# First norm of a hybrid decoder step: scale and shift weights by quarters of their features, early projection blocks a quarter of k at a time

## The chip, the core and the metric

The kernel runs on one core of a Trainium2 chip. The metric is device time in microseconds (us), from one execution; lower is better. Five engines work side by side, each through its own list of instructions in order: TensorE (PE, with its weight loads shown apart as PEld), VectorE (DVE), ScalarE (ACT), GpSimd (POOL) and SyncE (SP), which here only issues transfers (DMA) from HBM. They wait for one another by semaphores.

## The reference, cut to what matters

One step of a decoder trunk for 256 prompt tokens and 8 sequences of 4 sample tokens, 288 columns in all, with D = 2048 features. Only the beginning concerns this change:

```python
mod = jax.nn.silu(c) @ P['w_ada'] + P['b_ada']           # 9 conditioning vectors, 6 x 2048 outputs
sh1, sc1, gt1, sh2, sc2, gt2 = split(mod, 6)
xn = rmsnorm(x, P['g_norm1']) * (1.0 + sc1) + sh1
proj = xn @ P['w_in']                                     # 2048 x 13336, in f32
...                                                       # three recurrent branches, merge, MLP
```

## The kernel before

Features lie on the 128 partitions, so x is 16 k-tiles of 128 features by 288 columns. A product with a large weight goes through `stream`: per **granule** (two k-tiles by 512 output columns, 512 KB of weight) SP issues one load into a tile `raw`, ACT rounds it to `hi`, DVE forms `lo` = raw - hi, and PE runs 24 matmuls of 288 columns (hi with xh, hi with xl, lo with xh, over four column tiles and two k-tiles). `raw`, `hi` and `lo` have three tiles each. The normalized activations are kept in the same way as `xh` and `xl`.

The conditioning product `silu(c) @ w_ada` goes through `cond_product`: per **load** of 1 MB, PE runs small matmuls in four column groups at once into one PSUM tile `pa`; when all loads of a product are through, DVE transposes `pa` and adds the bias into `mod`. Six kinds of 16 MB each are needed: SC1 and SH1 (scale and shift of the first norm), GT1, SH2, SC2, GT2. Those after the first piece are **fillers**: `run` takes one step of the generator `fill` (one load) behind each granule of the projections, as `pace` says.

The order at the start, before the change:

- ACT's queue issues the four loads of x, SP's the first half of SC1 (8 loads, features of k-tiles 0 to 7).
- `modulate` writes x * rstd * SC1 for that half into two scratch slots and splits it into xh and xl.
- Three blocks of 512 output columns (NPRE = 3, the first of `B_Q`) run over k-tiles 0 to 7, 4 granules each, kept in `qk` and `vv`; meanwhile the second half of SC1 comes in as fillers.
- The same three blocks run over k-tiles 8 to 15 and are added by `plus_slot`; meanwhile SH1 (16 loads) comes in.
- These 24 granules use x without its shift. `shift` then rebuilds x from xh + xl on POOL, adds SH1 and splits it again, for all 16 k-tiles; and `shift_product` (16 loads of 768 KB, again fillers) adds sh1 @ w_in to what the three blocks gave.
- All other blocks use the shifted x.

The tile scheduler sets each engine's order from the program's dependences and priorities; SP issues in its listed order and waits when a tile is not free.

Of the kernel before, what the change touches and what calls it, by code (L numbers as in the profile page):

```python
# [14 lines left out]
P = 128  # L15
D = 2048
# [9 lines left out]
NPRE = 3  # blocks of the projections before sh1  # L26

# name -> width of the constant (by shape only) and parameter columns
# [19 lines left out]
# blocks of 512 columns in the packed input projection  # L48
# [4 lines left out]
def trunk(ctx, tc, io):  # L53
# [35 lines left out]
    # ---- constants, parameters  # L89
# [37 lines left out]

    # ---- streamed weights
# [3 lines left out]
    def weight_tile(kind):  # L132
        """1024 columns: of the kind's ring, or what stands in for it: a slot or a tile of the states' ring"""
# [12 lines left out]
    def stream(w, blk, act, kt, evac, g0=0, width=512, ahead=True, k0=0):  # L146
        """k-tiles k0..kt-1; act: k -> (hi, lo); generator with a step per granule"""
# [30 lines left out]
    # ---- conditioning: silu(c) @ w_ada + b_ada  # L178
    ct, th9 = (t288()[:, 0:KT * 9].rearrange("p (k c) -> p k c", k=KT) for _ in range(2))
    Q.dma_start(ct, io["ct"])  # L180
    S.activation(th9, ct, AF.Tanh, scale=0.5)
    V.scalar_tensor_tensor(th9, th9, 1.0, ct, ALU.add, ALU.mult)
    silc = cp.tile([P, KT * 9 + 23], F32, tag="silc", name="silc")  # 9 columns a k-tile; read 32 at a time
# [6 lines left out]
    def by_feature(ps, h, n):  # L190
        """up to eight k-tiles' columns from the column groups: k-tile, 32 columns"""
# [13 lines left out]
    def cond_product(load, each, cols, stat, finish):  # L205
# [3 lines left out]
        for q in range(KT // each):  # L209
            raw = raw_tile()  # L210
            load(raw, q)
            for i in range(each):
                k = each * q + i
                v = raw[:, cols * i:cols * i + cols].rearrange("p (m j f) -> p j m f", j=4, f=32)
                for j in range(4):
                    T.matmul(ps[32 * j:32 * j + 32, 0:cols // 4], stat(k), v[:, j], start=k == 0, stop=k == KT - 1)  # L216
            if q < KT // each - 1:
# [6 lines left out]
    def ada_finish(kind):  # L224
        def finish(h, pv):
            o = mod[:, kind, 8 * h:8 * h + 8, :]
            V.tensor_tensor(out=o, in0=pv[:, :, 0:9], in1=bada[:, kind, 8 * h:8 * h + 8].unsqueeze(2).to_broadcast([P, 8, 9]), op=ALU.add)
            if kind in (SC1, SC2):  # g * (1 + sc)
                gg = Pm("g1" if kind == SC1 else "g2")
                V.scalar_tensor_tensor(o, o, 1.0, gg[:, 8 * h:8 * h + 8].unsqueeze(2).to_broadcast([P, 8, 9]), ALU.add, ALU.mult)  # L230
# [7 lines left out]
    def ada(kind):  # L238
        def load(raw, k):
            Q.dma_start(raw.rearrange("p (h m) -> p h m", h=2), wada[kind, :, k].rearrange("h p m -> p h m"))  # L240
# [8 lines left out]
    def shift_product(dst, nb):  # L249
        """the tiles of dst += sh1 @ w_in's nb blocks, for each token by its sequence"""  # L250
# [13 lines left out]
        return cond_product(load, 1, 512 * nb, lambda k: modf[:, (SH1 * KT + k) * 9:(SH1 * KT + k) * 9 + 32], finish)  # L264
# [49 lines left out]
    def modulate(xg, rs, k0, fk, xh, xl, xr):  # L314
        """k-tiles k0..k0+3 of x (xg) -> hi and lo of x * rstd * f"""
        V.tensor_tensor(out=xr, in0=xg, in1=rs.unsqueeze(1).to_broadcast([P, 4, N]), op=ALU.mult)
        bc = [P, 2, NB, TS]
        for j in range(0, 4, 2):
            r = slice(k0 + j, k0 + j + 2)
            for i in range(j, j + 2):  # L320
                V.tensor_scalar(xr[:, i, 0:NP], xr[:, i, 0:NP], mod[:, fk, k0 + i, 0:1], None, ALU.mult)
            xs = smp(xr[:, j:j + 2])
            G.tensor_tensor(out=xs, in0=xs, in1=mod[:, fk, r, 1:9].unsqueeze(3).to_broadcast(bc), op=ALU.mult)
# [937 lines left out]
```

## Time and profile before

| | us |
|---|---|
| median of 3 runs | 2063.42 |
| lowest to highest | 2063.12 to 2064.65 |
| profiled execution, its own time (span from first to last instruction) | 2058.2 |
| PE busy in it | 2000.3 (97%) |
| PE matmuls of the granules on the chain that ended last (three lines) | 24%, 23%, 23% |
| DVE, ACT, POOL busy | 1031.4, 802.4, 302.0 |

The profiled execution shows a span of 2058.2 us; the median of the runs is 5.2 us longer, since it also holds what lies around the first and the last instruction. A busy PE in this profile is not a PE at its peak: a matmul waiting in the array for its neighbour counts as busy. The stretch from 0 to 250 us is the one in which the first norm and its weights are worked on.

### The profile page before, as it was taken

How to read it: one execution, taken by the hardware profiler on the slowest of the kernel's cores; microseconds unless marked ns; L12 is line 12 of the kernel's file. 1: busy time of each engine (PE TensorE's matmuls, PEld its weight loads, DVE VectorE, ACT ScalarE, POOL GpSimd, SP SyncE). 2: the span in 40 equal slices, each digit the busy share in tenths (PEclk: the TensorE clock that was granted, in tenths of full speed). 3: DMA queues.
4: the chain of work that ended last, by engine and by line, in shares of the span. 5: the costliest groups of instructions: out<-in, count | busy, mean ns of one | idle time of the engine just before them, and what ended most of it. 6: DMA issues, size and time to landing. Idle time of an engine off the chain costs nothing.

```text
span 2058.2 us, 35340 instructions
## 1 busy us (share of the span) xinstructions
PE 2000.3 (97%) x14834; PEld 1824.4 (89%) x14834; DVE 1031.4 (50%) x1406; ACT 802.4 (39%) x1099; POOL 302.0 (15%) x342
## 2 busy tenths in 40 slices
PE   6999999999999999999999999999999999999997
PEld 4778778877889788889998989999999999999997
DVE  4354655354644366454444465434545444454565
ACT  3323465332435332244333344444343434343434
POOL 0120111021202223101111242101010101010102
PEclk8999999999999999999999999999999999999999
DMA  9988685377663257777778755555555555555552
GB/s 386 356 316 308 207 298 180 132 243 265 213 235 126 83 187 233 250 251 272 246 252 303 235 187 162 166 170 166 166 163 167 167 166 164 166 165 168 166 167 98
DMA packets 120959, 429.60 MB, mean 209 GB/s; under 512 B 11600, under 2 KB 13808, under 8 KB 120672
## 3 DMA queue, kind: packets, MB, share of 16 engines
q1 hardware_dynamic: 111728, 393.59, 56.4%
q0 software_dynamic: 7920, 29.04, 4.0%
q10 hardware_dynamic: 1152, 4.72, 0.6%
q8 instruction: 116, 1.90, 0.4%
q14 instruction: 43, 0.35, 0.0%
HBM read 410.49 MB, written 16.81 MB: 208 GB/s over the span
## 4 chain that ended last, share of the span: by engine, by line
PE 78%; DMA 2%; DVE 1%; issue 1%; POOL 1%; ACT 0%; DVEq 0%; SPq 0%; POOLq 0%
PE mm L161 24%; PE mm L163 23%; PE mm L162 23%; PE pa L216 3%; DMA st<-mC 1%; DMA ag<-wada 1%; DVE lo L155 0%; PE px L658 0%; PE pi L974 0%; PE px L931 0%; PE pi L535 0%; PE px L125 0%; PE px L980 0%; PE px L555 0%; DMA o_C_s<-st 0%
## 5 line engine op out<-in xcount | busy, mean ns | idle before, releaser
L155 DVE TENSOR_TENSOR lo<-raw,hi 128x1024 fp32r<-128x1024 f32 (+1 forms) x424 | 543.0, 1283 | 616.9 <-ACT hi L154 603.7
L154 ACT ACTIVATE hi<-raw 128x1024 fp32r<-128x1024 f32 (+1 forms) x424 | 442.9, 1046 | 801.5 <-PE mm L162 663.2
L161 PE MATMUL mm<-xh,hi 128*128 128x288 f32 x2168 | 645.4, 300 | 12.0 <-ACT xh L341 5.5
L162 PE MATMUL mm<-xl,hi 128*128 128x288 f32 x2168 | 641.3, 297 | 1.2 <-DVE xl L342 1.2
L163 PE MATMUL mm<-xh,lo 128*128 128x288 f32 x2168 | 630.2, 297 | 1.2 <-DVE lo L155 1.2
L161 PEld LDWEIGHTS mm<-xh,hi 128*128 128x128 f32 x2168 | 406.9, 188 | 67.5 <-issue 37.8
L163 PEld LDWEIGHTS mm<-xh,lo 128*128 128x128 f32 x2168 | 404.6, 189 | 13.4 <-issue 8.1
L162 PEld LDWEIGHTS mm<-xl,hi 128*128 128x128 f32 x2168 | 408.5, 188 | 8.8 <-issue 6.9
L162 PE MATMUL mm<-s,hi 128*128 128x288 f32 x1176 | 348.1, 296 | 0.0
L161 PE MATMUL mm<-s,hi 128*128 128x288 f32 x1176 | 347.6, 297 | 0.0
L163 PE MATMUL mm<-s,lo 128*128 128x288 f32 x1176 | 345.0, 295 | 0.0
L161 PEld LDWEIGHTS mm<-s,hi 128*128 128x128 f32 x1176 | 220.6, 188 | 13.6 <-issue 11.8
L163 PEld LDWEIGHTS mm<-s,lo 128*128 128x128 f32 x1176 | 220.9, 188 | 2.4 <-issue 2.2
L162 PEld LDWEIGHTS mm<-s,hi 128*128 128x128 f32 x1176 | 221.3, 188 | 1.2 <-issue 0.9
L1102 POOL TENSOR_TENSOR t<-t 128x288 f32<-128x288 f32 x64 | 62.6, 989 | 638.9 <-ACT t L1101 638.9
L161 PE MATMUL mm<-s,st 128*128 128x288 f32 x488 | 143.9, 296 | 0.0
L162 PE MATMUL mm<-s,st 128*128 128x288 f32 x488 | 143.3, 294 | 0.0
L154 ACT ACTIVATE st<-s 128x1024 fp32r<-128x1024 f32 x80 | 84.7, 1059 | 131.0 <-PE mm L162 86.9
L161 PE MATMUL mm<-xh,st 128*128 128x288 f32 x408 | 120.5, 297 | 0.2 <-DVE xl L1088 0.2
L162 PE MATMUL mm<-xl,st 128*128 128x288 f32 x408 | 120.1, 295 | 0.0
L161 PEld LDWEIGHTS mm<-s,st 128*128 128x128 f32 x488 | 91.7, 188 | 0.8 <-ACT t L296 0.8
L162 PEld LDWEIGHTS mm<-s,st 128*128 128x128 f32 x488 | 91.9, 188 | 0.0
(369 smaller groups left out, 2104.6 us busy)
## 6 DMA issues: line engine op xcount, KB each, us to landing
raw<-win SPq DMA_DIRECT2D x192, 512.0 KB, 4.4
raw<-wf SPq DMA_DIRECT2D x176, 512.0 KB, 3.4
ag<-wada SPq DMA_DIRECT2D x57, 1024.0 KB, 6.1
s<-wf SPq DMA_DIRECT2D x80, 512.0 KB, 3.5
s<-wada SPq DMA_DIRECT2D x39, 1024.0 KB, 8.3
raw<-wout SPq DMA_DIRECT2D x32, 512.0 KB, 4.4
s<-win SPq DMA_DIRECT2D x11, 768.0 KB, 7.2
st<-mC POOLq DMA_DIRECT2D x16, 514.0 KB, 4.6
```

The lines of the kernel that those rows point to most:

```text
L154: S.activation(hi, raw, AF.Copy)
L155: V.tensor_tensor(out=lo, in0=raw, in1=hi.bitcast(F32), op=ALU.subtract)
L161: T.matmul(pss[m][:, :N], hi[:, kk, ms], xh, start=k == k0, stop=False)
L162: T.matmul(pss[m][:, :N], hi[:, kk, ms], xl, start=False, stop=False)
L163: T.matmul(pss[m][:, :N], lo[:, kk, ms], xh, start=False, stop=k == kt - 1)
L216: T.matmul(ps[32 * j:32 * j + 32, 0:cols // 4], stat(k), v[:, j], start=k == 0, stop=k == KT - 1)
L1102: G.tensor_tensor(out=r, in0=r, in1=r, op=ALU.mult)
```

## The change

- The weights of SC1 and SH1 are stored anew (`wada1`) and multiplied by quarters of their output features: one product is 4 loads, each of four k-tiles by 512 features, 128 columns a matmul, and each partition's row of a load is 8 KB in one piece. The order is SC1 q0; SC1 q1; SC1 q2, SH1 q2; SC1 q3, SH1 q3; SH1 q0; SH1 q1.
- x is loaded on SP's queue ahead of the weights, and is multiplied by rstd in place, all four quarters at once.
- `modulate(q)` scales quarter q in place and, in quarters 2 and 3 (`LATE` = 2 and up), adds the shift in the same pass.
- The three early blocks run over k a quarter at a time: 2 granules for each block, 6 for a quarter. Quarters 1 to 3 are added by `plus_slot`.
- `shift(q)` is left for quarters 0 and 1 and works on x in place; POOL's sum of xh and xl is gone. `shift_product` runs over k-tiles 0 to 7 alone: 8 loads, not 16.
- An extra activation `warm` on ACT at the start; GT1, SH2, SC2 and GT2 get a plain layout (8 KB rows).

```diff
+    xa, xb = slot(0), slot(1)
+    xq = [(xa, xb)[q // 2][:, 4 * (q % 2):4 * (q % 2) + 4, :] for q in range(4)]
     Q.dma_start(ct, io["ct"])
+    for q in range(4):
+        Q.dma_start(xq[q], io["x"][:, 4 * q:4 * q + 4, :])
...
+    S.activation(sc([P, 1], "warm", 1), eps, AF.Sqrt)
...
-    def ada_half(kind, h):
-        """eight of the k-tiles of one kind"""
-        def load(raw, q):
-            Q.dma_start(raw.rearrange("p (k m) -> p k m", k=2), wada[kind, h, 2 * q:2 * q + 2].rearrange("k p m -> p k m"))
-        return cond_product(load, 2, 1024, silu_c, lambda _, pv: ada_finish(kind)(h, pv))
+    def ada_quarter(kind, q):
+        def load(raw, g):
+            Q.dma_start(raw, io["wada1"][kind, q, g])
+        return cond_product(load, 4, 512, silu_c, lambda _, pv: ada_finish(kind, 4)(q, pv))
...
     def fillers():
-        yield from ada_half(SC1, 1)
-        done.add("sc")
-        yield from ada(SH1)
+        for q in range(1, 4):
+            yield from ada_quarter(SC1, q)
+            if q >= LATE:
+                yield from ada_quarter(SH1, q)
+            modulate(q)
+            done.add(q)
+        for q in range(LATE):
+            yield from ada_quarter(SH1, q)
+            shift(q)
         done.add("sh")
-        yield from shift_product((qk, vv), NPRE)
+        yield from shift_product((qk, vv), NPRE, 4 * LATE)
...
-    def shift(k0, shk, xh, xl, xr):
-        h, l = xh[:, k0:k0 + 4, :], xl[:, k0:k0 + 4, :]
-        G.tensor_tensor(out=xr, in0=h.bitcast(F32), in1=l.bitcast(F32), op=ALU.add)
+    def shift(q):
+        k0, x = 4 * q, xq[q]
+        with tc.high_priority():
+            by_seq(x, SH1, k0, ALU.add)
...
-    for i in range(4):
-        t = (xa, xb)[i // 2]
-        S.dma_start(t[:, 4 * (i % 2):4 * (i % 2) + 4, :], io["x"][:, 4 * i:4 * i + 4, :])
...
-    slots["ids"] = 2, 4, 5, 6, 7, 8, 9, None
-    all_of(ada_half(SC1, 0))
-    xs3, xs4 = slot(3), slot(4)
+    slots["ids"] = 2, 3, 4, 5, 6, 7, None
...
+    all_of(ada_quarter(SC1, 0))
+    modulate(0)
...
-    for b in range(NPRE):
-        run(stream(win, B_Q + b, act1, 8, to_slot((qk, vv)[b // 2], 4 * (b % 2)), ahead=b > 0))
-    drain("sc")
-    scale1(1)
-    for b in range(NPRE):
-        run(stream(win, B_Q + b, act1, KT, plus_slot((qk, vv)[b // 2], 4 * (b % 2)), k0=8))
+    for q in range(4):
+        if q:
+            drain(q)
+        for b in range(NPRE):
+            ev = plus_slot if q else to_slot
+            run(stream(win, B_Q + b, act1, 4 * q + 4, ev((qk, vv)[b // 2], 4 * (b % 2)), ahead=q > 0, k0=4 * q))
     drain("sh")
-    for i in range(4):
-        shift(4 * i, SH1, xh, xl, (xs3, xs4)[i % 2][:, 0:4, :])
```

What this makes of the order shows at three places. The first is SP's queue at the start. The destinations are `s..` (a slot), `ag` (the ring tile) and `raw`. Before:

```order
L180 DMA t288_1_89<-ct 128x144
L246 DMA s4_24_159<-wada 128x2x1024
...
L246 DMA ag_30_219<-wada 128x2x1024
L246 DMA s2_31_229<-wada 128x2x1024
L153 DMA raw_41_275<-win 128x1024
L153 DMA raw_46_316<-win 128x1024
```

and after:

```order
L185 DMA s0_1_89<-x 128x1152 x2
L185 DMA s1_2_90<-x 128x1152 x2
L257 DMA s3_27_167<-wada1 128x2048
...
L257 DMA s6_30_221<-wada1 128x2048
L154 DMA raw_36_258<-win 128x1024
L257 DMA s7_40_289<-wada1 128x2048
L154 DMA raw_41_307<-win 128x1024
L257 DMA ag_44_341<-wada1 128x2048
L154 DMA raw_49_363<-win 128x1024
```

Four loads of weights, not eight, now stand ahead of the first granule's `raw`, and x stands ahead of all of them.

The second is PE's list where the thirteenth granule of the early blocks begins (`pa` is the conditioning product; the first `mm` rows are the granule). Before, it follows the fifth load of SH1:

```order
L163 MATMUL mm_82_615<-xh1_104,lo_98_727 128x288
L216 MATMUL pa_86_646<-s2_99_759,silc_94 32x512 x4
L216 MATMUL pa_86_646<-s5_107_821,silc_94 32x512 x4
L161 MATMUL mm_100_787<-xh1_104,hi_105_792 128x288
L162 MATMUL mm_100_787<-xl1_105,hi_105_792 128x288
```

and after:

```order
L164 MATMUL mm_100_797<-xh1_106,lo_107_848 128x288
L225 MATMUL pa_152_1278<-s7_161_1331,silc_102 32x128 x11
L225 MATMUL pa_152_1278<-ag_165_1383,silc_102 32x128 x16
...
L225 MATMUL pa_178_1497<-s5_191_1602,silc_102 32x128 x16
L225 MATMUL pa_178_1497<-s6_192_1620,silc_102 32x128 x16
L162 MATMUL mm_112_930<-xh1_106,hi_117_935 128x288
```

All 32 loads of SC1 and SH1 now stand ahead of the thirteenth granule on PE; before, 21 stood ahead of it (16 of SC1, 5 of SH1) and 11 of SH1 behind it. On SP the same place reads, after:

```order
L257 DMA s5_191_1602<-wada1 128x2048
L257 DMA s6_192_1620<-wada1 128x2048
L154 DMA raw_116_934<-win 128x1024
L154 DMA raw_120_982<-win 128x1024
```

The granule's `raw` (`raw_116`) is the 48th transfer of the list and follows the last load of SH1.

The third is POOL's list where the shift is made. Before:

```order
L329 TENSOR_TENSOR s3_33_243<-xh1_104,xl1_105 128x1152
L329 TENSOR_TENSOR s4_34_244<-xh1_104,xl1_105 128x1152
L425 DMA s5_263_2108<-lst 128x192
L333 TENSOR_TENSOR s3_33_243<-s3_33_243,mod_97 128x4x32
...
L446 DMA s3_261_2105<-lruw 128x2048
```

and after:

```order
L334 TENSOR_TENSOR s1_2_90<-s1_2_90,mod_105 128x4x32 x4
L334 TENSOR_TENSOR s0_1_89<-s0_1_89,mod_105 128x4x32
L460 DMA s3_298_2495<-lruw 128x2048
L439 DMA s5_300_2498<-lst 128x192
L334 TENSOR_TENSOR s0_1_89<-s0_1_89,mod_105 128x4x32
```

The sums of 1152 columns are gone, and the 1 MB load `lruw` now stands between the shift of quarter 0 and that of quarter 1.

## Rows read from the trace of the kernel before

**Rows 1.** The page: PE's line (busy us, share, instructions) and the granted clock in 40 slices.

```profile
PE 2000.3 (97%) x14834; PEld 1824.4 (89%) x14834; DVE 1031.4 (50%) x1406; ACT 802.4 (39%) x1099; POOL 302.0 (15%) x342
...
PEclk8999999999999999999999999999999999999999
```

**Rows 2.** Stretches: us, busy (instructions) of PE, PEld, DVE, ACT, POOL, clock, DMA, GB/s.

```profile
10.00:20.00 10.00, 8.47 (x69) 4.96 (x69) 3.06 (x19) 5.16 (x11) 0.00 (x0) 1.00 1.02 411
20.00:30.00 10.00, 5.53 (x66) 2.57 (x68) 4.58 (x3) 0.50 (x1) 0.00 (x0) 0.91 1.02 408
30.00:40.00 10.00, 3.87 (x32) 1.60 (x24) 6.44 (x15) 5.50 (x7) 2.90 (x6) 0.50 1.02 408
40.00:50.00 10.00, 8.85 (x62) 7.96 (x60) 5.28 (x7) 0.07 (x1) 0.00 (x0) 0.74 1.02 409
...
46.00:97.00 51.00, 51.00 (x433) 39.59 (x431) 18.03 (x26) 18.44 (x28) 8.93 (x6) 1.00 0.96 358
```

**Rows 3.** Instructions in order of time: start, us, engine, line, what, [idle before <-releaser].

```profile
32.79 1.06 ACT L154 ACTIVATE hi<-raw 128x1024 fp32r<-128x1024 f32 x1 [10.89 <-DMA raw<-win]
...
38.98 1.33 PE L161 MATMUL mm<-xh,hi 128*128 128x288 f32 x4 [5.51 <-ACT xh L341]
...
50.56 1.06 ACT L154 ACTIVATE hi<-raw 128x1024 fp32r<-128x1024 f32 x1 [10.49 <-DMA raw<-win]
```

**Rows 4.** Stretches from granule to granule, all instructions, columns as in rows 2.

```profile
38.97:97.18 58.21, 57.05 (x456) 45.12 (x456) 24.52 (x33) 19.71 (x30) 8.93 (x6) 0.95 0.96 363
97.19:137.96 40.77, 40.77 (x308) 30.95 (x305) 15.45 (x24) 7.97 (x8) 2.52 (x4) 1.00 0.97 368
137.97:245.86 107.89, 105.40 (x794) 93.22 (x793) 60.04 (x75) 42.04 (x55) 14.01 (x15) 1.00 0.72 238
198.81:208.40 9.59, 9.59 (x74) 9.59 (x73) 3.68 (x3) 3.19 (x3) 0.00 (x0) 1.00 0.53 165
```

**Rows 5.** The first three of them for line L216 alone: PE, PEld, clock, DMA, GB/s.

```profile
38.97:97.18 58.21, 14.64 (x168) 4.36 (x168) 0.95 0.96 363
97.19:137.96 40.77, 11.17 (x92) 2.04 (x88) 1.00 0.97 368
137.97:245.86 107.89, 13.81 (x120) 3.41 (x120) 1.00 0.72 238
```

**Rows 6.** PE's waits between 138 and 170 us, columns as in rows 3.

```profile
147.36 0.40 PE L163 MATMUL mm<-xh,lo 128*128 128x288 f32 x1 [0.82 <-DVE lo L155]
...
153.00 0.37 PE L161 MATMUL mm<-xh,hi 128*128 128x288 f32 x1 [1.18 <-DVE s L380]
...
168.82 0.40 PE L161 MATMUL mm<-xh,hi 128*128 128x288 f32 x1 [0.46 <-ACT hi L154]
```

**Rows 7.** The shift on POOL and DVE, columns as in rows 3.

```profile
141.37 3.58 POOL L329 TENSOR_TENSOR s<-xh,xl 128x1152 f32<-128x1152 f32 x1 [3.13 <-DVE xl L342]
...
142.34 3.83 DVE L342 TENSOR_TENSOR xl<-s,xh 128x1152 fp32r<-128x1152 f32 x1
```

**Rows 8.** Transfers issued from 0 to 160 us: count, KB each, median us to landing.

```profile
s<-wada SPq DMA_DIRECT2D x26, 1024.0 KB, 8.9
raw<-win SPq DMA_DIRECT2D x30, 512.0 KB, 7.7
...
s<-x ACTq DMA_DIRECT2D x4, 576.0 KB, 7.4
...
con<-con POOLq DMA_DIRECT2D x1, 422.0 KB, 6.8
par<-par POOLq DMA_DIRECT2D x1, 213.0 KB, 6.7
```

**Rows 9.** Queues from 20 to 28 us, then 160 to 170: packets, MB, engines' share.

```profile
q1 hardware_dynamic: 837, 3.24, 101.3%
...
q0 software_dynamic: 144, 1.05, 25.0%
```

**Rows 10.** Groups by line, 96 to 160 us: count | busy us, mean ns | idle before.

```profile
L380 DVE TENSOR_TENSOR s<-s,mm 128x288 f32<-128x288 f32 x12 | 5.2, 450 | 13.2 <-PE mm L163 12.9
```

More of the change, by code (lines that the diff above doesn't have):

```diff
@@ L26 @@
 NPRE = 3
+LATE = 2
 CONSTS = [("ident", 128), ("eye", 32), ("bcol", 8), ("smask", 32), ("slo", 32), ("shi", 32),
@@ L176, in run @@
                 next(fill, None)
-    ct, th9 = (t288()[:, 0:KT * 9].rearrange("p (k c) -> p k c", k=KT) for _ in range(2))
+    xa, xb = slot(0), slot(1)
+    xq = [(xa, xb)[q // 2][:, 4 * (q % 2):4 * (q % 2) + 4, :] for q in range(4)]
+    ct = t288()[:, 0:KT * 9].rearrange("p (k c) -> p k c", k=KT)
     Q.dma_start(ct, io["ct"])
+    for q in range(4):
+        Q.dma_start(xq[q], io["x"][:, 4 * q:4 * q + 4, :])
+    th9 = t288()[:, 0:KT * 9].rearrange("p (k c) -> p k c", k=KT)
     S.activation(th9, ct, AF.Tanh, scale=0.5)
+    S.activation(sc([P, 1], "warm", 1), eps, AF.Sqrt)
     V.scalar_tensor_tensor(th9, th9, 1.0, ct, ALU.add, ALU.mult)
@@ L203, in raw_tile, with cond_product @@
         return flat(slot(i))[:, 0:2048]
-    def cond_product(load, each, cols, stat, finish):
+    def cond_product(load, each, cols, stat, finish, kt=KT):
         ps = pa.tile([P, 512], F32, tag="pa", name=nm("pa"))
-        for q in range(KT // each):
+        for q in range(kt // each):
             raw = raw_tile()
@@ L215, in cond_product @@
                 for j in range(4):
-                    T.matmul(ps[32 * j:32 * j + 32, 0:cols // 4], stat(k), v[:, j], start=k == 0, stop=k == KT - 1)
-            if q < KT // each - 1:
+                    T.matmul(ps[32 * j:32 * j + 32, 0:cols // 4], stat(k), v[:, j], start=k == 0, stop=k == kt - 1)
+            if q < kt // each - 1:
                 yield
@@ L263, in finish @@
             G.tensor_tensor(out=d, in0=d, in1=o[:, :, 1:9].unsqueeze(3).to_broadcast([P, n, NB, TS]), op=ALU.add)
-        return cond_product(load, 1, 512 * nb, lambda k: modf[:, (SH1 * KT + k) * 9:(SH1 * KT + k) * 9 + 32], finish)
+        return cond_product(load, 1, 512 * nb, lambda k: modf[:, (SH1 * KT + k) * 9:(SH1 * KT + k) * 9 + 32], finish, kt)
     def all_of(g):
@@ L312, in smp @@
         return a[..., NP:N].rearrange("p k (b t) -> p k b t", b=NB)
[L314 to L323, printed above, removed]
-            split(xh[:, r, :], xl[:, r, :], xr[:, j:j + 2])
@@ new lines, in modulate @@
+    def modulate(q):
+        k0, x = 4 * q, xq[q]
+        with tc.high_priority():
+            by_seq(x, SC1, k0, ALU.mult)
+            if q >= LATE:
+                by_seq(x, SH1, k0, ALU.add)
+            for j in range(0, 4, 2):
+                for i in range(j, j + 2):
+                    f, sh = (mod[:, kind, k0 + i, 0:1] for kind in (SC1, SH1))
+                    if q >= LATE:
+                        V.tensor_scalar(x[:, i, 0:NP], x[:, i, 0:NP], f, sh, ALU.mult, ALU.add)
+                    else:
+                        V.tensor_scalar(x[:, i, 0:NP], x[:, i, 0:NP], f, None, ALU.mult)
+                r = slice(k0 + j, k0 + j + 2)
+                split(xh[:, r, :], xl[:, r, :], x[:, j:j + 2])
@@ L336, in split @@
+    def shift(q):
+        k0, x = 4 * q, xq[q]
+        with tc.high_priority():
+            by_seq(x, SH1, k0, ALU.add)
+            for i in range(4):
+                V.tensor_scalar(x[:, i, 0:NP], x[:, i, 0:NP], mod[:, SH1, k0 + i, 0:1], None, ALU.add)
+            split(xh[:, k0:k0 + 4, :], xl[:, k0:k0 + 4, :], x)
     def split(dst_h, dst_l, src):
@@ L360, in trunk @@
     rs = rstd_of(ps)
+    for q in range(4):
+        V.tensor_tensor(out=xq[q], in0=xq[q], in1=rs.unsqueeze(1).to_broadcast([P, 4, N]), op=ALU.mult)
     def act1(k):
@@ L381, in plus_slot @@
         return f
-    def scale1(h):
-        t = (xa, xb)[h]
-        for i in range(2):
-            with tc.high_priority():
-                modulate(t[:, 4 * i:4 * i + 4, :], rs, 8 * h + 4 * i, SC1, xh, xl, (xs3, xs4)[i % 2][:, 0:4, :])
-    slots["ids"] = 2, 5, 6, 7, None
-    scale1(0)
+    all_of(ada_quarter(SC1, 0))
+    modulate(0)
     G.tensor_copy(con[:, 0:1], mod[:, SC1, 0, 0:1])
@@ L394, in trunk @@
     pace["every"] = (1,)
[L395 to L400 removed]
+    for q in range(4):
+        if q:
[3 more added lines that the diff above has]
+            run(stream(win, B_Q + b, act1, 4 * q + 4, ev((qk, vv)[b // 2], 4 * (b % 2)), ahead=q > 0, k0=4 * q))
     drain("sh")
[L402 to L403 removed]
     pace["every"] = (1, 0)
```

25 lines of the change are left out of this document (12 added, 13 removed).

## The prediction

> **What bounds the kernel now.** I read the page first: PE is busy 97% of the span and the granted clock stands below 9 only in the first of the 40 slices [rows 1]. So nothing can come back except idle PE time, slow-clock time, or PE work that is left out. Next the stretches [rows 2]. From 10 to 50 us the DMA column stands at 1.02 and 408 to 411 GB/s while PE is half idle at 20 to 40 and the clock goes down from 0.91 to 0.50: the start waits for transfers. From 46 to 97 us PE is busy in all 51.00 us and DMA runs at 358 GB/s, below what it has just shown: now PE is the bound. The first granule begins at 38.98, after 5.51 us of idleness [rows 3]. From there to 97.18 the weight loads number 456, of which 168 are the conditioning product's [rows 4, 5]; 288 are left, twelve granules of 24. So the thirteenth granule begins at 97.19, and I use it as the milepost: what comes after it is nearly the same in both kernels, and what PE still owes there can be counted.
>
> **What one piece costs.** Three granules without fillers take 9.59 us, 3.20 each [rows 4]. From 97.19 to 137.96 there are nine granules (28.8 us) and 88 weight loads of the product, 8 for a load of SH1, so 11 loads [rows 4, 5]: (40.77 - 28.8) / 11 = 1.09 us of PE each. From 137.97 to 245.86 there are 28 granules (89.5 us), 15 loads of the shift product, and the three waits of 0.82, 1.18 and 0.46 us [rows 4 to 6]: (107.89 - 89.5 - 2.5) / 15 = 1.06 us each.
>
> **Transfers.** The landing of a transfer in a saturated queue can be counted by bytes. Before, the first `raw` has behind it x and c (2.43 MB), the parameters (0.22), eight loads of 1.05 and its own 0.52 [rows 8], 11.56 MB; at 0.409 MB/us that is 28.3 us, and ACT takes it up at 32.79 [rows 3]: 4.5 us on top. The `raw` of 50.56 [rows 3] has 18.81 MB: 46.0 + 4.5 = 50.5. So landing = 4.5 + MB / 0.409, as long as SP never lets the queue run dry.
>
> **The change, part by part.**
>
> *A smaller first piece.* Four loads instead of eight ahead of the first granule. The fifth load (first of SC1 q1) stands ahead of it on PE, 8.4 MB, lands at 25; with its 1.09 us and the scaling, the first granule begins at about 27, 12 us earlier. This is no gain yet.
>
> *The milepost moves to the transfers.* Ahead of the thirteenth granule PE now owes twelve granules and 27 loads after the first granule's start: 38.4 + 29.4 = 68 us, so PE could be there at 95. But the granule's `raw` is the 48th transfer, behind all 32 loads: 2.43 + 0.22 + 0.43 + 32 x 1.05 + 13 x 0.52 = 43.45 MB, 106.2 + 4.5 = 110.7, and with 1.06 us of ACT [rows 3] 111.8. The transfers are later by some 16 us, and they decide; all that the early part does on PE, DVE, ACT or POOL (extra activation, smaller transposes, seven ends of products that wait for DVE) lies in those 16 us and costs nothing unless it exceeds them.
>
> *Two corrections to 111.8.* The new loads have one row of 8 KB a partition. The only such load in the trace took 25.0% of 10 us for 1.05 MB, 2.50 us, where those of the first half of SC1 took 101.3% of 8 us for 3.24 MB, 2.62 per load [rows 9]: between 0 and 32 x 0.12 = 3.8 us earlier; I take 2, since the row is of POOL's queue. And `lruw` (1.05 MB) now goes out between the shifts of q0 and q1, when the last loads are still under way: between 0 and 2.6 us later; I take 1. So the thirteenth granule begins at 110.8 (108 to 114.5).
>
> *What PE no longer owes there.* Before, at 97.19, there were still 11 loads of SH1 (12.0 us), 16 of the shift product, of which 8 are dropped (8.5 us), and the waits of 2.5 us. The first two of these lie where DVE is held up: the xl of 1152 columns takes 3.83 us beside POOL's sum of 3.58 [rows 7]; the sums are gone, so I count all three waits as gone. The same state is reached before at 97.2 + 12.0 + 8.5 + 2.5 = 120.2.
>
> *New waits behind the milepost.* 24 more additions by `plus_slot` at 0.45 us [rows 10] are 10.8 us of DVE work, on an engine half idle, but PE's next block needs the PSUM tile that they empty. The `raw` of the sixteenth granule can be issued only when the thirteenth's `lo` is made, and lands about when PE wants it. No row shows these; the nearest are the waits of 0.46 to 1.18 us [rows 6]. Bounds 0 and 4 us; I take 2.0.
>
> *Sum.* 120.2 - 110.8 - 2.0 = 7.4 us. Everything later has the same granules and fillers and I cost it at nothing. Against the profiled execution: 2058.2 - 7.4 = 2050.8. The median of the runs is 5.2 us above that execution's span, so 2063.4 - 7.4 = **2056.0**.
>
> **The clock.** The trace shows the granted clock at 0.50 (the 1.2 GHz level) at 30 to 40 us, after PE had been busy 5.53 of 10 us, and 0.74 at 40 to 50, when the granules ran without a gap [rows 2]. Now PE waits for transfers between 27 and 111, with 68 us of work in 84. Slow work there eats the 16 us of slack first. The Trainium skill ("TensorE: Matmul & The Clock Gate", section "HAM oscillation — how this bites in real kernels") says that a kernel whose bursts of matmuls are shorter than the waits for data between them starts every burst at the low clock. By that rule the pieces of this stage would each run at half speed; the trace agrees for the one such stretch that it has, and it is the third rival.
>
> **The rivals.**
>
> 1. *The queue has holes and the gain is given back.* SP issues in order, and a load waits for its tile; with seven tiles the twenty-sixth load waits for PE to finish the nineteenth. By my count SP is some 12 us ahead there, so the queue should not run dry, but the trace before does show 358 GB/s as soon as tiles bind [rows 2]. At a mean of 390, 43.45 MB take 111.4 us, the milepost is at 117.0, the gain 1.2: 2062.
>
> 2. *Slower: the holes are as before.* If this stage gets the 358 GB/s of 46 to 97 us [rows 2], the milepost is at 121.4 + 4.5 + 1.1 = 127.0 and the kernel 8.8 us slower: 2072. It decides from 43.45 / (118.2 - 5.6), 386 GB/s, downwards. Against it: 40 us on end at 408 and more, with the same sizes. The Trainium skill ("DMA: Bandwidth & Descriptors", section "Where 436 GB/s comes from") gives about 358 GB/s as HBM's limit for one core and says that it binds transfers from HBM; by it the time would be the same 2072. The rows of 10 to 50 us exceed it, so it adds little to the chance.
>
> 3. *PE at half clock.* If the clock stays at half for more than about 16 us of PE work (at full clock) between 27 and 111, PE decides the milepost and not the transfers; and if it is down at the milepost, the granules there take 6.4 us instead of 3.2 until it is back. Slack used up and 3 us more at each end: about 2066. For it: the busy share of 20 to 30. Against: work of 68 in 84 us, and a PE that falls behind is a PE without gaps.
>
> **How the numbers follow.** Forecast 0.70 (2051 to 2060), rival 1 0.16, rival 2 0.09, rival 3 0.05. A measurement of this kernel tells some 0.2%, 4.1 us, from no change. Faster than 2059.3: nearly all of the forecast and a third of rival 1, 0.74. Within 0.2%: most of rival 1, some of the forecast and of rival 3, 0.13. Slower: rival 2 and the rest, 0.13. The range runs from all corrections in favour (milepost 108, no new waits: 12 us, 2051) to rival 1, 2050.5 to 2063.
>
> **What would show it.** Right: the first granule near 27; DMA above 400 GB/s from 10 to about 105; the thirteenth granule near 111 and its `hi` released by DMA, with PE idle or product-only in the 10 us ahead; three waits of [rows 6] gone, no sum on POOL. Wrong: GB/s below 390 in that stretch (rivals 1, 2); a clock under 0.9 from 50 to 110 (rival 3); waits of PE behind DVE of more than 4 us between 111 and 250.

## The result: slower, and the profile after

The median of 20 runs is 2070.0 us, against 2063.6 for 20 runs of the kernel before on the same chip: the ratio is 1.0033 with an interval of 1.0020 to 1.0046, about 6.8 us slower. The forecast was 2056.0, and faster. The profiled execution of after has a span of 2060.8 us and took 2062.6, so 1.8 us lie around the span, and it is one of the shortest of its set. Against the 2058.2 of before it is 2.6 us longer. Both numbers are needed below: 2.6 us between the two traces, and between the sets of runs 6.4 by the medians or 6.8 by the ratio.

The page, to be held against [rows 1]: PE's line and the granted clock.

```profile
PE 1997.6 (97%) x15410; PEld 1846.6 (90%) x15410; DVE 1034.8 (50%) x1430; ACT 804.4 (39%) x1099; POOL 286.4 (14%) x334
...
PEclk9999999999999999999999999999999999999999
```

PE is busy 2.7 us less, in a span that is longer. The start is no longer slow. Stretches with the columns of [rows 2]:

```profile
20.00:30.00 10.00, 5.33 (x73) 4.64 (x74) 9.55 (x15) 3.27 (x4) 1.29 (x3) 0.76 1.02 419
...
46.00:97.00 51.00, 42.65 (x650) 38.18 (x651) 23.15 (x41) 14.37 (x21) 1.99 (x4) 1.00 1.02 417
...
46.00:110.00 64.00, 52.42 (x884) 46.97 (x888) 27.68 (x51) 15.53 (x22) 3.65 (x7) 1.00 1.02 417
110.00:120.00 10.00, 6.83 (x51) 6.56 (x40) 5.82 (x10) 4.34 (x4) 0.74 (x2) 0.66 1.03 392
```

From 46 to 97 us, where PE had been busy all the time, it is now busy 42.65 of 51 us and the transfers run at 417 GB/s, faster than in any row of [rows 2]. At the milepost the clock is at half: 0.66 is the mean of 10 us in which it stood at 0.50 from 110.6 to 117.4. The first granule, the thirteenth, and the `hi` for which the latter waits, as in [rows 3]:

```profile
27.69 0.61 PE L162 MATMUL mm<-xh,hi 128*128 128x288 f32 x1 [0.42 <-ACT xh L367]
...
112.43 1.06 ACT L155 ACTIVATE hi<-raw 128x1024 fp32r<-128x1024 f32 x1 [6.21 <-DMA raw<-win]
...
113.54 0.61 PE L162 MATMUL mm<-xh,hi 128*128 128x288 f32 x1 [3.17 <-ACT hi L155]
```

The chain is as forecast (transfer, `hi`, granule, PE idle ahead of it), 2.7 us later. How SP issues these transfers, in order of time (start, us, operation, tile, count):

```profile
60.24 9.11 SPq L257 DMA_DIRECT2D s<-wada  x5
70.28 4.04 SPq L154 DMA_DIRECT2D raw<-win  x3
...
82.09 7.30 SPq L257 DMA_DIRECT2D s<-wada  x5
90.24 5.30 SPq L154 DMA_DIRECT2D raw<-win  x3
```

Loads and granules stand in **bursts**: five or more loads, then three granules (three `raw` tiles), then loads again. The code is written with one load between two granules; the order came out this way because the loads have seven tiles and the granules three. So all 32 loads stand ahead of the thirteenth granule, which the prediction knew and counted. What it did not weigh is what bursts do to PE: it waits for a load, then works them all off, then waits for a `raw`. Waits of PE from 46 to 120 us (who for whom, us in all, times, longest):

```profile
PE mm L162 <- ACT hi L155: 6.5, 4, 3.2
PE pa L225 <- DMA s<-wada: 5.3, 4, 1.8
PE pa L225 <- DVE s L347: 1.5, 1, 1.5
```

And granule to granule for all instructions, then for the product's line alone, as in [rows 4] and [rows 5]:

```profile
113.53:254.98 141.45, 141.44 (x1008) 124.28 (x1009) 74.09 (x110) 48.70 (x62) 8.56 (x13) 0.99 0.68 233
...
113.53:254.98 141.45, 19.46 (x120) 3.81 (x120) 0.99 0.68 233
```

From the thirteenth to the fiftieth granule (254.99; before 97.19 to 245.87) PE never waits: the waits of [rows 6] and the sum of [rows 7] are gone. But 37 granules of 3.20 are 118.4 us, and 120 weight loads of the product are 15 loads, so these took (141.45 - 118.4) / 15 = 1.54 us each, where before they took 1.07.

### The profile page after: what moved, and what is told of

Its sections match the earlier page's. It is cut to its first block, busy times and chain, and to the rows that moved or that the text cites. A ratio compares the mean times of both kernels' runs of the same rounds, so it can differ in the third digit from the quotient of the medians.

```text
span 2060.8 us, 36520 instructions
## 1 busy us (share of the span) xinstructions
PE 1997.6 (97%) x15410; PEld 1846.6 (90%) x15410; DVE 1034.8 (50%) x1430; ACT 804.4 (39%) x1099; POOL 286.4 (14%) x334
## 4 chain that ended last, share of the span: by engine, by line
PE 89%; DMA 5%; DVE 2%; issue 2%; ACT 1%; POOL 1%; DVEq 0%; SPq 0%; POOLq 0%; ACTq 0%
PE mm L162 27%; PE mm L164 26%; PE mm L163 26%; PE pa L225 4%; DMA raw<-win 3%; DMA st<-mC 1%; DVE lo L156 1%; DMA ag<-wada 1%; DMA s<-wada 1%; PE pi L381 1%; PE px L672 0%; PE px L945 0%; PE pi L549 0%; PE pi L988 0%; ACT hi L155 0%
```

## How runs are compared

Two runs of one kernel differ by 15 us and more, and each run's record holds its span and its mean granted clock. Span times clock estimates what the run would have taken at 2.4 GHz throughout; the rest of the span is put down to stretches at 1.2 GHz. That splits a mean over runs into two parts. The split is rough. Within one kernel span times clock still spreads by 2.4 us (standard deviation over all sets), where the spans spread by 3.6. And it counts half clock at which PE has nothing to do: in each profile 3.9 to 5.4 us of the loss lie in the last 8 to 11 us, behind PE's last matmul, and cost nothing. All ratios are to the kernel before on the same chip. "Steps" and "tiles" are explained with the experiments.

| kernel | ratio, interval | mean span | lost to clock | at full clock |
|---|---|---|---|---|
| before (four sets of 23 to 35) | 1 | 2059.9 to 2062.3 | 19.8 to 21.3 | 2040.1 to 2040.9 |
| before_again | 1.0005, 0.9992 to 1.0018 | 2061.0 | 20.6 | 2040.4 |
| after | 1.0033, 1.0020 to 1.0046 | 2067.8 | 24.5 | 2043.3 |
| after_again | 1.0028, 1.0016 to 1.0040 | 2066.0 | 23.4 | 2042.6 |
| late4 | 1.0036, 1.0020 to 1.0052 | 2066.4 | 20.7 | 2045.7 |
| warm1 | 1.0048, 1.0030 to 1.0065 | 2069.8 | 21.7 | 2048.1 |
| tiles3 | 1.0001, 0.9986 to 1.0015 | 2060.2 | 24.4 | 2035.8 |
| steps8 | 1.0010, 0.9997 to 1.0024 | 2061.5 | 21.3 | 2040.2 |
| tie | 1.0018, 1.0001 to 1.0035 | 2063.9 | 20.8 | 2043.1 |
| mix | 0.9983, 0.9970 to 0.9995 | 2056.1 | 23.3 | 2032.8 |
| mix_tie | 0.9974, 0.9957 to 0.9991 | 2055.6 | 19.2 | 2036.4 |
| lruw_late | 1.0012, 0.9998 to 1.0026 | 2063.1 | 23.7 | 2039.4 |
| mix_late4 | 0.9963, 0.9950 to 0.9977 | 2053.3 | 13.9 | 2039.5 |
| mix8 | 0.9933, 0.9914 to 0.9952 | 2047.5 | 20.5 | 2027.0 |
| mix8, second set | 0.9926, 0.9900 to 0.9952 | 2046.9 | 18.4 | 2028.5 |
| steps_gt2 | 1.0015, 1.0003 to 1.0028 | 2065.6 | 22.0 | 2043.5 |
| norm_warm | 1.0030, 1.0017 to 1.0043 | 2068.2 | 23.6 | 2044.6 |

A difference of 1 to 1.5 us in a part of a row is within what sets of the same kernel show (2040.1 to 2040.9 and 19.8 to 21.3 for before, 2042.6 and 2043.3, 23.4 and 24.5 for after; the two sets of six runs of mix8 differ by 2.1 in the clock). Between after and before, 1.7 to 3.2 us are work and waits and 2.1 to 4.7 are clock, as the sets are paired; after_again and the before beside it on one chip give 2.5 and 3.6.

## The experiments

### The two kernels once more

before_again and after_again have no edit.

> The kernel before, unchanged, run again for its own spread and for a second profile. Medians so far: before 2063.6 us, after 2070.0 us. Clock theory: the runs of after differ from one another by their mean granted clock (0.984 gave 2076, 0.991 gave 2061.7 to 2067.8), and the profiled run of before had 0.991; so before's runs should lie near 0.990 to 0.991 in the mean, after's near 0.988, and at equal clock the two kernels should differ by less than 2 us. Rival, later waits: the clocks are alike, and after is some 6 us longer at equal clock. Second profile: no stretch at half clock between 90 and 130 us nor between 300 and 360 us, if the ones of after belong to after.

> The kernel after, unchanged, beside the others of this call: is it as long on this chip, and does its clock loss come again? Spans of after so far: 2067.8 us in the mean at a mean granted clock of 0.9881, of before 2060.4 at 0.9904; span times (1 - clock) is what half speed costs: 24.5 us for after, 19.8 for before, so 4.7 us of the 7.4 us between them is clock and 2.8 us is work and waits. If that belongs to the kernel: 2068 to 2071.5 us, clock 0.987 to 0.989, and a wait of 4.2 us near 1223 us, with no load beside it. If it belonged to the chip and the hour: within 2 us of before.

Measured: 2063.3 us at a mean clock of 0.9900, and 2068.2 at 0.9887. The slowdown belongs to the kernel. At full clock the two are 1.7 to 3.2 us apart: the clock theory (under 2) has the larger part of the difference, but not all of it. The second profile of before has no half-clock stretch from 90 to 130 or 300 to 360 us, as expected; the second of after has them again at 111, 309 and 347 us.

### late4: the second part of the change undone

```diff
-LATE = 2
+LATE = 4
```

> The kernel after with the shift in none of the quarters: all of it goes through the product of the shift with the blocks, 16 loads of that product instead of 8. The prediction's price for the 8 loads is 8 x 1.06 = 8.5 us of TensorE; with after at 2070.0 us it gives 2076 to 2080 us, the 13th granule within 2 us of 113.5 us, since the same 32 loads stand ahead of it. Rival, the second part is hidden or is given back later in waits: 2068 to 2073 us.

Measured: 2067.4 us, ratio 1.0036, thirteenth granule at 112.74. The rival holds: eight more loads of the shift product make after no longer by anything that can be measured in the total. By the table late4 is 2.4 to 3.1 us longer at full clock and loses 2.7 to 3.8 us less to the clock. What the prediction counted as 8.5 us isn't there in this kernel's time, and the first part of the change alone is 7 us slower than before.

### tiles3 and mix: no bursts

tiles3 gives the loads three tiles instead of seven; mix gives the first four loads tiles of their own, and those behind them three.

```diff
-    slots["ids"] = 2, 3, 4, 5, 6, 7, None
+    slots["ids"] = 4, 5, 6, 7
...
     all_of(ada_quarter(SC1, 0))
+    slots["ids"] = 2, 3, None
```

> The kernel after with three tiles instead of seven for the loads of the scale, shift and shift product while the early blocks run: the program's row then has about one load between two granules, and only some 14 loads ahead of the 13th granule instead of 32. Bunching theory (loads queued in bursts of five to seven ahead of the granules' own weights make the stretch to 113 us bound by transfers): the 13th granule between 78 and 95 us, no wait for a load over 2 us between 50 and 90, and 2045 to 2058 us in all, faster than both kernels. Clock theory alone (only half-clock stretches cost): the half-clock stretch at the milepost goes, 2 to 5 us less than after, 2064 to 2068 us. Later-stage theory (the loss is behind 250 us, whatever comes ahead): 2067 to 2073 us, with the same half-clock stretches near 310 and 350 us after the shift in time.

> As tiles3, but the four loads of the first scale quarter have four tiles of their own, and the loads behind them three: tiles3's first granule started at 34.3 us instead of 27.7, since its fourth load waited for a tile. Bunching theory: first granule at 27.5 to 28.5, no burst of loads, the 13th granule at 82 to 88, and 5 to 6.5 us less than tiles3 (2062.9): 2056 to 2058.5 us. Rival (transfers bind after all once the start is earlier, 28 transfers ahead of the 13th granule at 413 GB/s would be there by 70 us): 2060 to 2063 us.

Measured: tiles3 2062.9 us, thirteenth granule at 91.20; mix 2058.0, at 86.04, first granule at 28.5. SP now issues in single file. The lines are those of mix8, below, which has mix's order here:

```profile
56.23 0.33 SPq L154 DMA_DIRECT2D raw<-win  x1
59.70 0.33 SPq L257 DMA_DIRECT2D ag<-wada  x1
60.12 0.86 SPq L154 DMA_DIRECT2D raw<-win  x2
64.87 3.92 SPq L257 DMA_DIRECT2D s<-wada  x2
```

At full clock mix stands 10 us below after, and the forecast gain of 7.4 us over before is there (2032.8 against 2040.4). And mix begins its fiftieth granule at 246.17, 8.8 us ahead of after, with the same loads left to do. So the bursts are one cause, and the larger one. The edit changes two things together, the waits between bursts and the number of loads ahead of the milepost (17 instead of 32), and no run tells these apart. tiles3's expected time was missed by 5 us, since its fourth load waits for a tile and its first granule starts at 34.34; mix mends that and gains the 5 us, as expected. But mix still loses 23.3 us to the clock, as after does: single file doesn't cure that.

### warm1: is it the clock at the milepost?

One product of 288 columns that nothing reads, behind each of the last 16 loads:

```diff
+            if warm:
+                T.matmul(misc()[:, :N], ones, raw[:, 0:N], start=True, stop=True)
```

> The kernel after with one more product of 128x128 with 288 columns, whose result nothing reads, behind each of the last 16 loads of the scale and shift (16 x about 0.5 = 8 us of TensorE, in a stretch of 46 us that holds about 36 us of work). Clock theory: no half-clock stretch at 110 to 117 us, the 13th granule within 2 us of 113.5, and 2 to 4 us less than after by 160 us; in all 2064 to 2069 us if the later stretches stay as they are. Rival, the clock there doesn't depend on how busy TensorE was, or the extra products delay the granules: half clock all the same, 2070 to 2076 us. Bunching theory: the milepost itself doesn't move, since transfers bound it.

Measured: 2072.1 us, thirteenth granule at 112.33. The half-clock stretch at the milepost is gone; another comes at 134.6, behind a new wait:

```profile
110.00:120.00 10.00, 9.38 (x101) 7.63 (x93) 7.28 (x13) 4.16 (x4) 1.46 (x3) 1.00 1.03 399
130.00:140.00 10.00, 6.78 (x32) 4.69 (x33) 2.84 (x6) 0.94 (x1) 0.00 (x0) 0.83 0.97 344
```

The loss to the clock falls by some 2 us and the time at full clock rises by 5, so the expected gain did not come; the median lies in the rival's range. The milepost itself is where the bytes put it.

### lruw_late: the bytes ahead of the milepost

A copy of one column holds the LRU's weights back:

```diff
+        G.tensor_copy(flat(wax)[:, 0:1], flat(lx)[:, 0:1])
         G.dma_start(flat(wax)[:, 0:2048], io["lruw"])
```

> The kernel after with the transfer of the LRU's weights (1.05 MB, which runs beside the loads on POOL's queue ahead of the 13th granule) held back until the LRU's projection is out, by a copy of one column. Size theory: the milepost is bound by the sum of the bytes, so the 13th granule starts 2 to 2.6 us earlier, at 110.8 to 111.5 instead of 113.5 us, and the median falls by no more than that, 2067 to 2070 us. Rival (that transfer doesn't compete): 113.5 and the time of after within 1 us.

Measured: thirteenth granule at 111.44, 2.1 us earlier than in after and 1.3 earlier than in after_again; the size theory holds there. The median is 2064.1, ratio 1.0012, some 3 to 4 us below after, more than expected. In its profile PE waits 1.35 instead of 3.17 us at the milepost and no half-clock stretch follows there. But another one stands at 64.9 to 71.7, and over its runs the loss to the clock is that of after (23.7); the table has the 3 to 4 us at full clock (2039.4). What makes up more than the 2.1 us stays open.

### steps8 and steps_gt2: where the later loads stand

The eight dropped loads leave a row that is shorter by eight: every later load (GT1, SH2, SC2, GT2) stands eight granule steps earlier than before. steps8 puts eight empty steps in their place and changes no work; steps_gt2 puts them only ahead of GT2.

```diff
         done.add("cor")
+        for _ in range(8):
+            yield
```

> The kernel after with eight empty steps in the row of fillers, behind the shift product and ahead of the loads of the later scales: the loads that follow stand at the granules at which they stood in the kernel before, which had eight loads more ahead of them. Nothing of the work changes. Later-stage theory (the dropped loads pull the later ones forward, onto the stage of the LRU, and the waits and half-clock stretches of after between 300 and 355 us come from that): the waits on DVE L533 fall from 3.33 and 3.01 us to the 2.2 and 2.5 us of before, the half-clock stretches near 308 to 319 and 350 us go, and the median is 2062 to 2066 us. Rival (the stage's waits don't depend on where the loads stand): 2068 to 2072 us.

> The kernel after with the eight empty steps of steps8 only ahead of the loads of the last scale, so that everything up to some 900 us stands as in after, and only the second norm near 1220 us has loads again beside its wait. steps8 took 5.3 to 7 us off after; this tells its two parts apart. Cover theory (the loads are missing at the second norm): the wait there falls from 4.2 us to some 2.7, with 2.8 loads beside it, 2.0 to 2.5 us at full clock and up to 3.4 us of clock: 2063 to 2066.5 us. Rival (the stage of the LRU and the GLA, 290 to 600 us, had the gain, by where the loads stand there): 2067 to 2070 us.

Measured: steps8 2062.9 us, ratio 1.0010, 4 to 5 us below after, as expected; but not where I expected it. Its waits from 285 to 360 us, in the LRU's stage, fell only from 7.4 to 6.2 us in all: PE waited 3.9 us behind DVE at 295 us, with a half-clock stretch behind it. What the traces show is the second norm. Before, PE's row there (start, us, instructions, [idle before]):

```profile
1215.34 0.63 PE L216 MATMUL pa<-s,silc 128*32 128x512 f32 x3
1215.36 0.62 PE L216 MATMUL pa<-ag,silc 128*32 128x512 f32 x1
1215.79 0.61 PE L216 MATMUL pa<-s,silc 128*32 128x512 f32 x3
1215.81 1.44 PE L216 MATMUL pa<-ag,silc 128*32 128x512 f32 x7
...
1218.26 1.62 PE L300 MATMUL pi<-t,ones 128*128 128x288 f32 x6
1222.36 1.56 PE L216 MATMUL pa<-ag,silc 128*32 128x512 f32 x8 [2.48 <-DMA ag<-wada]
1224.08 1.33 PE L161 MATMUL mm<-xh,st 128*128 128x288 f32 x4 [0.15 <-DVE xl L1088]
```

and after:

```profile
1219.17 0.75 PE L317 MATMUL pi<-t,ones 128*128 128x288 f32 x2
...
1220.64 1.24 PE L317 MATMUL pi<-t,ones 128*128 128x288 f32 x4 [0.23 <-ACT t L313]
1222.35 0.75 PE L317 MATMUL pi<-t,ones 128*128 128x288 f32 x2 [0.47 <-ACT t L313]
1227.31 1.33 PE L162 MATMUL mm<-xh,st 128*128 128x288 f32 x4 [4.21 <-ACT xh L1101]
```

Before, 22 matmuls of the product (2.75 loads) stood around the norm's chain of ACT and DVE, and PE waited 2.6 us; after, the loads had run out before it, and PE waited 4.9 us with nothing else to do. The code says so: ahead of the norm it asks for three more loads, and after the change there are none left to give. In steps8 they are back, and PE waits 2.7 us. The dropped loads had been **cover** for this wait.

steps_gt2 restores just that: the 22 matmuls are back and PE waits 2.41 us. Its median is 2068.6 us, in the rival's range (the kernel before had 2063.5 on that chip). By its ratio, 1.0015, it is some 3 us below after, the size that the cover theory gave; yet the split by clock puts none of it at full clock (2043.5), and the interval touches that of after. (The 5.3 to 7 us for steps8 in its expectation are differences of medians from different chips; by the ratios they are 4 to 5.) So the row shows 2.3 to 2.5 us at the norm; how much of it reaches the end, and what the rest of steps8 is, stays open.

### tie and mix_tie: the waits of the LRU's stage

Waits of PE from 290 to 360 us, in before and then in after:

```profile
PE mm L161 <- DVE s L519: 4.8, 2, 2.5
```

```profile
PE mm L162 <- DVE s L533: 6.3, 2, 3.3
PE px L593 <- DMA s<-wg: 1.1, 1, 1.1
```

DVE's four scans of 1.34 us stand in a row ahead of the next `lo` and of the instruction of L533 that PE waits for, in after:

```profile
302.43 5.09 DVE L513 TENSOR_TENSOR_SCAN s<-s,s 128x576 f32<-128x576 f32 x4
```

tie holds them back with copies of one column until granules of the gate are out:

```diff
+                V.tensor_copy(flat(hh)[:, 2 * h * N:2 * h * N + 1], (sm[:, 0:1], sg[:, 0, 0:1], sg[:, 4, 0:1], sg[:, 4, 0:1])[h])
                 V.tensor_tensor_scan(flat(hh)[:, r], flat(aa)[:, r], flat(thi)[:, r], 0.0, ALU.mult, ALU.add)
```

> The kernel after with the four scans of the LRU (1.34 us of DVE each, in one row ahead of the lo of the next granules) held back by copies of one column until granules of the gate have come out, so that the lo stands between them. It tests what the waits at 305 and 345 us cost, with their half-clock stretches. Clock theory (the half-clock stretches at 308 to 319 and 350 us follow from these waits): both waits under 1 us, the stretches gone, 2043.3 us at full clock fall by 4 to 6 and the loss of clock of 24.5 us by some 5: 2059 to 2063 us. Rival (half-clock stretches come elsewhere instead): the waits go alone, 2064 to 2067 us. Second rival (the scans only delay something else as much): 2068 to 2072 us.

> mix and the held-back scans of tie together. If the bursts of loads and the waits of the LRU stage are two separate causes, their gains add: mix's 5 to 6.5 us below tiles3 and some 4 to 11 us for the scans, 2046 to 2054 us, faster than both kernels. If the clock takes back what the waits gave, 2055 to 2058 us, as mix alone.

Measured: tie 2066.1 us, mix_tie 2057.9. The stretch is cured:

```profile
300.00:320.00 20.00, 20.00 (x139) 14.79 (x138) 12.68 (x23) 5.66 (x8) 1.12 (x2) 1.00 0.80 302
...
365.00:380.00 15.00, 13.10 (x91) 12.02 (x90) 9.05 (x7) 10.18 (x16) 4.23 (x3) 0.89 0.57 209
```

PE is busy 20.00 of 20 us at full clock where after had two half-clock stretches. But a new wait of 1.9 us, with a half-clock stretch, stands at 366, and the time at full clock is that of after (2043.1); only the loss to the clock is 3 us less. For mix the scans bring nothing: 4 us less clock, 4 us more work and waits. The two expectations of a full gain fell; tie came out where the first rival had it (stretches come elsewhere instead), mix_tie at mix alone.

### mix8 and mix_late4: both mended, and the price of the dropped loads

mix8 is mix with the eight empty steps, mix_late4 is mix with LATE = 4.

> mix (loads not in bursts) with the eight empty steps of steps8 (the loads of the later scales stand where before had them). mix alone: 2058.0 us, of which 2032.8 us at full clock and 23.3 us lost to the clock; it waits 4.2 us at the second norm (1217 to 1222 us) with no load left there, where before had 22 weight loads of the product in the same stretch and waited 2.5 us. Cover theory (loads that were dropped had covered waits further on): 2.3 us less wait there, and the clock loss back towards 20 us: 2051 to 2056 us, faster than all others. Rival (the two edits mend the same loss): 2057 to 2059 us.

> mix with the whole shift through the product with the blocks, 16 loads instead of 8: the price of the second part of the change where no burst and no transfer hides it. A whole load of that product takes 0.78 us of TensorE in the traces, so 8 are 6.2 us, or up to 8 us where they stand cut in pieces; less the 2.3 us that they cover at the second norm: 2061 to 2064 us at mix's clock. Rival (as with late4 against after, the loads cost nothing in the sum): 2056 to 2059 us.

> mix8 once more, word for word, for an interval of its own: its first set held only six runs. If the gains of the loads in single file and of the eight steps add, 2047 to 2051 us, some 13 us below before and 20 below after, at a clock loss near 20.5 us as in before; if the first set was a lucky one, 2052 to 2056 us.

(The last of these ran mix8 unchanged, as its text says; the label names another edit.) Measured: mix8 2048.7 and 2049.8 us, ratios 0.9933 and 0.9926: **14 us faster than before and some 20 faster than after**, the best of all. mix_late4 is 2055.8, ratio 0.9963, 5 us below what I expected, just under the rival's range. The same product, eight loads more or less, has these prices:

- later loads eight steps too early: late4 to after, 1.0036 to 1.0033 and 1.0028, and mix_late4 to mix, 0.9963 to 0.9983: from 1.6 us gained to 4 us lost;
- later loads in their place: late4 to steps8, 1.0036 to 1.0010, and mix_late4 to mix8, 0.9963 to 0.9933 and 0.9926: 5.4, 6.2 and 7.6 us gained.

So the second part of the change is worth 5 to 8 us, near its forecast, but in the total only if what follows keeps its place. Where it does not, the clock takes the gain: at full clock the pairs of the first line give 2.4, 3.1 and 6.7 us gained, those of the second 5.5, 11.0 and 12.5. And mix differs from mix_late4 in more than the place of later loads. Its profile has a wait of 3.0 us for a load at 112.7, with half clock from 115.0 to 121.8 behind it; mix_late4's is busy 68.49 of the 70 us from 60 to 130, all at full clock. PE's waits in mix8 from 50 to 130 us, to be held against after's above:

```profile
PE pa L225 <- DVE s L349: 1.5, 1, 1.5
PE pa L225 <- DVE t L202: 0.9, 1, 0.9
PE pa L225 <- DMA s<-wada: 0.8, 1, 0.8
PE mm L162 <- ACT xh L369: 0.8, 1, 0.8
```

### norm_warm: does filling a wait save clock?

Five products that nothing reads, behind the second norm's reciprocal:

```diff
+    for _ in range(5):
+        T.matmul(misc()[:, :N], ones, rs, start=True, stop=True)
```

> The kernel after with five products of 128x128 with 288 columns, whose result nothing reads, behind the second norm's reciprocal, in its wait of 4.2 us (5 x 0.62 = 3.1 us): TensorE has something to do there, but no work is saved. Clock theory (the half-clock stretch at 1227 us follows from the idle time ahead of it): no half-clock stretch between 1220 and 1235 us, 1.7 to 3.4 us less lost to the clock, 2065 to 2068 us. Rival (what the idle time does to the clock is small or the half-clock stretch comes elsewhere): 2068 to 2071 us.

Measured: 2070.4 us, ratio 1.0030, as after. PE still waits 2.58 us, for the reciprocal, and the clock is down from 1231.0 all the same:

```profile
1228.27 0.75 PE L317 MATMUL pi<-t,ones 128*128 128x288 f32 x2 [0.46 <-ACT t L313]
...
1231.61 1.81 PE L1088 MATMUL px<-row,ones 128*128 128x288 f32 x3 [2.58 <-DVE row L325]
```

The median lies in the rival's range, and the clock theory gets nothing from this run; since part of the wait stayed, it isn't refuted either.

## Why the prediction was wrong, step by step

**The first granule, the rate, the chain: right.** Near 27 was forecast, 27.69 came. The transfers were to run above 400 GB/s from 10 to 105; they ran at 413 to 422 (stretches of 10 us, and 417 from 46 to 110). At that rate a load with 8 KB rows comes to 1.05 MB / 417 GB/s = 2.51 us, as the row of POOL's queue had shown [rows 9]. Rivals 1 and 2 fell with it: the queue had no holes. The page that spoke for rival 2, the Trainium skill's "DMA: Bandwidth & Descriptors", section "Where 436 GB/s comes from", gives about 358 GB/s as the limit of HBM for one core; the trace has 417 over 51 us, and the measurement decides.

**"So the thirteenth granule begins at 110.8": 2.7 us too early.** 113.54 lies inside the bounds that stood beside it (108 to 114.5). Holding `lruw` back gave 2.1 against after and 1.3 against after_again (112.75): that transfer took half or more of the possible 2.6, where I had counted 1.

**"Slow work there eats the 16 us of slack first": right up to the milepost, then wrong.** The third rival's second half came true at the worst place: the clock was at 0.50 from 110.6 to 117.4, just when the granules began. From 113.54 on that is 3.86 us at half, 1.9 us lost. Of the page of the Trainium skill named there, "TensorE: Matmul & The Clock Gate", section "HAM oscillation — how this bites in real kernels", the trace bears out no more than this stretch: from 46 to 110 us PE was idle 11.6 of 64 us, in waits between bursts, and the clock was 1.00. That 1.00 is in part this profile's luck: late4, steps8, lruw_late, steps_gt2 and norm_warm load in the same bursts there, and each has 3.4 to 6.8 us at half clock between 65 and 73 us. The prediction named the case that came (the clock down at the milepost), but it gave both halves of the rival one price, 2066, and one chance, 0.05, and none of it stands in the sum.

**"12.0 and 8.5 us", loads at 1.07 us each whatever their place: the term that failed most.** The 15 loads between the thirteenth and the fiftieth granule took 23.05 us instead of 16.05. Half clock is 1.9 of it. Another 4.7 come from loads that are **cut**. A piece of after's product, and the granule matmul behind it, twice; then a whole load in tiles3:

```profile
137.79 0.84 PE L225 MATMUL pa<-s,mod 128*32 128x384 f32 x4
138.56 0.40 PE L162 MATMUL mm<-xh,hi 128*128 128x288 f32 x1
...
139.81 0.83 PE L225 MATMUL pa<-s,mod 128*32 128x384 f32 x2
140.57 0.40 PE L162 MATMUL mm<-xh,hi 128*128 128x288 f32 x1
```

```profile
166.07 0.85 PE L225 MATMUL pa<-ag,mod 128*32 128x384 f32 x8
166.86 0.40 PE L162 MATMUL mm<-xh,hi 128*128 128x288 f32 x1
```

Half a load (4 matmuls), a quarter (2) and a whole one (8) each hold PE for 0.76 to 0.79 us: the four column groups run side by side, and a piece with one of them lasts as long as all four. Added up from such starts, after's 15 loads took 18.3 us (1.22 each). Before's 26 took 25.4, of which 1.6 are the last two waits of [rows 6], which stand behind pieces; that leaves 23.7 (0.91 each). The price of 1.06 to 1.09 in the prediction was a mean over the cuts of before's order; in another order it is another price. lruw_late, with after's pieces here and no half clock, bears it out: 1.44 us a load, by the same sum over its 140.00 us. The remaining 0.4 us are the granules, which take more than 3.20 us where a piece stands in them, in both kernels, now shared by fewer loads.

**"New waits 2.0": none came.** PE does not wait between 113.54 and 254.99. That gives 2.0 back.

So at the fiftieth granule after was to stand at 110.8 + 2.0 + 118.4 + 16.05 = 247.3 and stands at 254.99: 7.7 us too late, 2.7 + 7.0 - 2.0. That alone is the whole forecast gain.

**"Everything later has the same granules and fillers and I cost it at nothing": wrong.** Later there are eight loads fewer, and I had counted them as saved without asking what they stood beside. From the fiftieth granule to the end before needs 1812.3 us and after 1805.8: 6.5 us less, where 8 x 1.06 = 8.5 were due. Up to PE's last matmul the stretches read:

```profile
245.87:2045.30 1799.43, 1776.03 (x13124) 1644.45 (x13122) 907.48 (x1220) 717.48 (x979) 267.74 (x303) 1.00 0.58 195
```

```profile
254.99:2047.90 1792.91, 1768.96 (x13060) 1645.86 (x13058) 901.89 (x1202) 719.19 (x979) 266.49 (x301) 1.00 0.57 191
```

The first is before, the second after. PE is idle 23.4 us in before and 24.0 in after, and 10.2 and 13.7 us of the stretches are at half clock, which loses 5.1 and 6.8. So 0.6 more waiting and 1.7 more lost to the clock make up the 2.0 that are missing. The waits at the second norm (4.9 instead of 2.6 us) and in the LRU's stage (7.4 instead of 4.8) did grow, but others shrank by nearly as much; in this pair of profiles the lost cover does not show in the sum. 7.7 and 2.0 are 9.7 of the 10.0 us by which the trace misses the sum (2.6 longer instead of 7.4 shorter).

**"The median of the runs is 5.2 us above that execution's span": a wrong reading.** The text ahead of the prediction puts the 5.2 us down to what lies around the first and the last instruction. Around the span lie some 1.8 us in each run of the record (1.7 to 2.2); the other 3.4 were the profiled execution's luck. It does not move the forecast difference, but it hid that runs of one kernel differ by 15 us with their clock.

**What the traces don't hold.** The medians differ by some 4 us more than the profiled executions, and the table puts that into the clock: 2.1 to 4.7 us more lost in after. Between the start and PE's last matmul, the half-clock stretches of after's two profiles stand behind waits at the milepost, in the LRU's stage and at the second norm, and in after_again at 850 us; before's two have them at the second norm and near 840 to 850. A wait does not settle it: those of 2.2 and 2.5 us in the LRU's stage are followed by half clock in late4 and mix_late4 and by none in both profiles of before. Taking one wait away moved a stretch (warm1, tie) or left it (norm_warm), and the loss of mix_late4 is the least of all (13.9) while mix has 23.3, with the same tiles and single file. What sets the sum of these stretches is **not settled** by these runs.

## What to carry to other kernels

Work that leaves a row of fillers takes its cover along and moves every later filler: before counting it as saved, look at what each dropped piece stood beside, and at where the later ones now stand; if the gain matters, put empty steps in its place and see. The number of tiles of each ring decides whether two streams on one queue run in single file or in bursts, whatever the program's text says; print the order and count the pieces. And a price per load taken from one order holds for that order alone.

## What the hardware showed beyond that

- A piece of the product with one column group costs PE as much as one with all four: 0.76 to 0.79 us for 2, 4 or 8 matmuls of 384 columns (starts of the rows above).
- One core read 417 GB/s over 51 us, most of it in rows of 8 KB.
- A mean granted clock lower by 0.001 is 2.1 us of this kernel by the split; within the sets of runs it goes with 1.8 us. The runs of after go from 0.984 (2076.2 us) to 0.991 (2062.6 us). Differences of 0.3% between kernels here are as much clock as work, and one profiled execution can hide them: those of before and after both had 0.991.
